# A hybrid decoder step on one core: a third bank for the scores, the sample spread evenly, and TensorE's order fixed to the order of emission

## The chip, the core and the metric

The kernel runs on one core of a Trainium2 chip. A core has five engines with instruction queues of their own: TensorE (PE, matrix products; its weight loads are listed as PEld), VectorE (DVE), ScalarE (ACT), GpSimd (POOL) and SyncE (SP, which here issues nearly all DMAs). PE writes into eight PSUM banks of 128 x 512 float32 values; VectorE and ScalarE read them. The metric is the time of one execution on the device in microseconds (us).

## What is computed

One inference step: a recurrent layer, shared keys and values made from its result, then one layer of forgetting attention. It is done for a prompt of 2048 new positions and for 8 samples of 8 new positions each that look back on 4096 cached positions in pages.

```python
def fox_block(q, k, v, cq, ck, q_pos, k_pos):
    s = jnp.einsum('bqhd,bkhd->bhqk', q, k).astype(jnp.float32) * (HEAD_DIM ** -0.5)
    s = s + jnp.swapaxes(cq, 1, 2)[:, :, :, None] - jnp.swapaxes(ck, 1, 2)[:, :, None, :]
    mask = k_pos[None, :] <= q_pos[:, None]
    s = jnp.where(mask[None, None], s, -jnp.inf)
    p = jax.nn.softmax(s, axis=-1)
    return jnp.einsum('bhqk,bkhd->bqhd', p.astype(v.dtype), v)
...
def run_group(...):
    x = x + rms_norm(recurrent_mixer(rms_norm(x, ...), ...), ...)
    k_new, v_new, logf_new = shared_kv(x, kv_norm, w_kv, b_f)
    ...
    x = x + rms_norm(fox_mixer(rms_norm(x, ...), k_all, v_all, cq, ck, ...), ...)
```

There are 16 heads of 64 values; the model is 1024 wide. The sample reads 8 x 32 pages of 128 rows, keys and values, from a pool through a page table.

## The kernel before

Three stages follow each other: the recurrent layer, the projections to keys, values, queries and gates, and the attention of the prompt with the output projection behind it. The first 1024 positions pass the first two stages, then the rest. Beside the later projections and the attention runs the *sample*, the attention of the eight samples over cached pages. It is cut into 16 turns (a batch entry and half of the heads); the first two are done early, the other 14 by the generator `beside`.

The attention of the prompt (`attention`) goes through 64 units of a head and 512 queries. A unit has one *score* step per 128 keys, 640 in all. A step has two matmuls into a bank named st (L1531, L1532), on the diagonal a third that adds the mask (L1534). ScalarE takes the exponential of the bank (L1540) into a tile p in SBUF. After four steps the *value products* (ops, L1551) add p times the values into a bank of their own; they are emitted two steps late. GpSimd adds the p tiles up for the sums (L104). The exponential needs the maximum of each query beforehand: *maxima* (sx, L1404) are scores computed ahead of time, from which VectorE takes the largest (L1406; L1408 on the diagonal). mrow is the row of maxima of a unit, and mps its transpose (L1421), which ScalarE writes into the unit's queries (qbt).

A sample turn loads eight groups of four key pages and eight of value pages (L1072; tile raw, four buffers, 1 MB each). VectorE transposes the keys (ktr, L1157), PE makes scores from them (dS, L1125; L1140 for the new rows), VectorE subtracts the decay and takes maxima. At the end of a turn's keys the maximum (dm) is transposed on PE (L1177, L1181), ScalarE takes exponentials (L1194), PE sums them (dsum, L1203), VectorE transposes them (sy, L1210), and SP stores them to DRAM (pd, L1215) and loads them in another layout (sx, L1216). Then the value products of the turn (dO, L1235; L1243 for the new rows) follow page by page, and dres (L1263) folds the result. Key pages of the next turn are emitted between the value pages of this one. (The tile sx of the sample and the bank sx of the maxima share a name.)

PSUM in the attention: two banks belong to the sample (d, for its scores and the small products of the softmax, and o, for dO), six to the attention: one for ops, two for st, three for sx, mps and the products of the sums.

What sets the order. The program emits instructions in one stream. `Side.along` interleaves two generators: for each unit of cost that the attention reports, the sample is advanced by `share` units. A scheduler then orders each engine's queue with a timeline of its own and may put a later emitted instruction ahead of an earlier one that it expects to wait. `together` keeps a group of matmuls behind the group's first; there is no order between groups. With these costs the sample's share along the attention is that of the projections, 0.28; what is then left is emitted behind the attention (`side.upto`).

Of the kernel before, what the change touches and what calls it, by code (L numbers as in the profile page):

```python
# [11 lines left out]
F32 = mybir.dt.float32  # L12
# [8 lines left out]
P = 128  # L21
# [6 lines left out]
H = 16  # L28
# [15 lines left out]
B_ORDER += [("g", c) for c in range(4)]  # L44

SHARE = 1.13
LEAD = 18
RAMP = 8
NS = 3
# [2 lines left out]
AHEAD = 8  # L52
FIRST = 2
NACC = 5
NP = 5
ADD = "G"
OG = 1
NQ = 6
# [14 lines left out]


SYNC = mybir.DependencyInfo(mybir.DependencyClass.Sync, mybir.DependencyReason.DATA)


def f(ap):
# [5 lines left out]
def tile_hawk_fox(  # L84
# [8 lines left out]
    V, A, G, T, S = nc.vector, nc.scalar, nc.gpsimd, nc.tensor, nc.sync  # L93
# [9 lines left out]
    def tt(eng, out, a, b, op):  # L103
        eng.tensor_tensor(out, a, b, op=op)  # L104

    def together(mms, after=()):

        first = mms[0]().ins
        for d in after:
            tc.add_manual_dep(first, d.ins.name, SYNC)  # L110
        with tc.high_priority(), tc.issue_after(first):
            for mm in mms[1:]:
                mm()


    xs_flat = x_sample.rearrange("b q d -> (b q) d")
# [94 lines left out]
    psum = {}  # L211
# [810 lines left out]
    def decode(es, turns, nraw, nktr, ahead):  # L1022
# [26 lines left out]
        last, qbs = [], {}  # L1049

        def bank(name, tag="d"):
            return psum["dec"].tile([P, 512], F32, name=name, tag=tag, bufs=1)

        def spare():
# [252 lines left out]
    def attention(es):  # L1307
# [86 lines left out]
        def top(u, j, ck):  # L1394

            h, qc = units[u]
            assert h in loaded and u < done[1]
            kb, qb = kbs[h % 2], qbs[u % NQ]
            if (j, ck) == (0, 0):
                mxs[u] = small.tile([P, 4, 4], F32, name="mxs", tag="mxs")  # L1400
            mx = mxs[u]
            w = 512 if ck < qc else (j + 1) * P
            ps = ps3.tile([P, 512], F32, name="sx", tag="sx", bufs=3)
            T.matmul(ps[:, :w], qb[0:96, j * P:(j + 1) * P], kb[0:96, ck * 512:ck * 512 + w], start=True, stop=True)  # L1404
            if ck < qc:
                V.reduce_max(mx[:, j, ck:ck + 1], ps[:, :w], axis=AX.X)  # L1406
            else:
                V.tensor_tensor_reduce(ps[:, :w], ps[:, :w], maskb[:, 512 - w:], scale=1.0, scalar=NEG,  # L1408
                                       op0=ALU.add, op1=ALU.max, accum_out=mx[:, j, ck:ck + 1])
            if j == 3 and ck == qc:  # L1410
                later.after(1, lambda: tops(u))
# [108 lines left out]
            yield 300  # L1520
        ops = acc = None
        pair = []
        for u, (h, qc) in enumerate(units):
            load_low(u + 2)
            for k in range(nks[u]):
# [1 line left out]
                qa, qb = qas[u], qbs[u % NQ]  # L1527
                lo = max(0, k - qc * 4) * P
                ks = slice(k * P, (k + 1) * P)
                ps = ps3.tile([P, 512], F32, name="st", tag="st", bufs=2)  # L1530
                T.matmul(ps[:, lo:], ka[:, ks], qa[:, lo:], start=True, stop=False)  # L1531
                T.matmul(ps[:, lo:], kb[:, ks], qb[:, lo:], start=False, stop=(k < qc * 4))  # L1532
                if k >= qc * 4:
                    T.matmul(ps[:, lo:lo + P], identB[:, :], causal[:, :], start=False, stop=True)  # L1534
# [38 lines left out]
                    load_head(h + 1)  # L1573
                yield 4.1 * (512 - lo) * 0.42 + (done[0] - before) * 213

    lent = {}

    rows = [(NSAMP, None, x1s_d[:, :], ys_flat)]
    rows += [(P, t, x1_d[t:t + P], yp_flat[t:t + P]) for t in range(SEQ - P, -1, -P)]
# [2 lines left out]
    def project_ready(es):  # L1582

        pool = sbuf(es, "projw", "right")
        proj["g"] = pool.tile([P, D], F32, name="bpostB")
        S.dma_start(proj["g"][:, :], b_post_norm.broadcast_to([P, D]))
        out = proj["out"] = Out(b_w_out[0], 0).place(pool)
        with ExitStack() as st:
            wpool["st"], wpool["ns"] = sbuf(st, "projs", "right"), 2
            out.fetch()  # L1590
            out.fetch()
            for i in range(8):
                yield 2000
                out.split(i + 1)
# [189 lines left out]
    def beside():  # L1784
        yield from decode(dec, turns[FIRST:], 4, 2, True)
        dec.close()
        yield from project_ready(last)

    side = Side(beside())
# [3 lines left out]
    wkeep.close()  # L1793
    lin.close()
    psum["att"] = banks(att, "psa", 6)
    side.along(attention(att), share)
    side.upto(1e12)
    project(last)
    att.close()
# [36 lines left out]
```

## Time and profile before

| | us |
|---|---|
| median of three runs | 3062.46 |
| runs | 3054.63 to 3064.86 |
| the profiled execution | 3055.27 |
| its span | 3053.6 |
| PE busy in the span | 2827.0 |
| VectorE busy | 1810.2 |
| ScalarE busy | 1269.8 |
| GpSimd busy | 1079.6 |
| attention, first score to last value product | 1725.5 to 2881.2 |
| first and last value product of the sample from 1690 us on | 1692.2 to 2559.9 |

The span runs from the first to the last instruction of one profiled execution. A row of a group gives line, engine, operation, output and inputs with shapes, the count, the busy time and the mean of one, and how long the engine was idle just before, with what ended that. PEclk is the granted share of PE's clock. Matmuls are pipelined, so the next one may start before the one ahead has ended; the distance from start to start tells what one costs. Line numbers are those of the kernel before; in the changed kernel those that the text names stand 16 to 31 lines further down: the scores' two matmuls are L1561 and L1563, the maxima L1420, the value products L1582, the sample's value products L1251.

### The profile page before, as it was taken

To read this page: it belongs to the slowest core of one execution; us is meant where nothing else is said; L and a number is where in the kernel's file an instruction comes from. 1 tells how busy PE (TensorE), PEld (TensorE's weight loads), DVE (VectorE), ACT (ScalarE), POOL (GpSimd) and SP (SyncE) were. 2 spreads that over 40 slices of the span, in tenths; PEclk is the share of its full clock that TensorE was granted. 3 is DMA by queue.
4 is the path that set the end of the run, shared out by engine and by line. 5 is a ranking of instruction groups with operands and counts; after the bars stand their busy time and mean duration, and the time that the engine had idled before them with its cause. 6 is when DMAs were issued, how large, how long until landed. Compare 5 with 4: busy or idle time off the path is not lost.

```text
span 3053.6 us, 60463 instructions
## 1 busy us (share of the span) xinstructions
PE 2827.0 (93%) x21614; PEld 2258.5 (74%) x21614; DVE 1810.2 (59%) x4012; ACT 1269.8 (42%) x2874; POOL 1079.6 (35%) x1199
## 2 busy tenths in 40 slices
PE   6998999999999989998999799899899899999898
PEld 5997789988999978896888456565556565565687
DVE  7876465425357766765555566676767675554344
ACT  4665442222346655433333144343444345455311
POOL 1653201000016532000000366556465557587522
PEclk9999999999999999999999799899999999999999
DMA  4224546788622256999999988999999998323243
GB/s 122 81 85 133 175 125 203 240 268 263 216 83 89 83 185 194 316 320 320 330 311 315 294 274 268 299 275 308 306 298 319 322 297 258 92 65 86 84 145 111
DMA packets 492864, 653.41 MB, mean 214 GB/s; under 512 B 91099, under 2 KB 292828, under 8 KB 485285
## 3 DMA queue, kind: packets, MB, share of 16 engines
q1 hardware_dynamic: 488934, 643.87, 67.1%
q10 hardware_dynamic: 3340, 3.56, 0.5%
q8 instruction: 171, 2.80, 0.4%
q0 software_dynamic: 288, 2.10, 0.2%
q14 instruction: 131, 1.07, 0.1%
HBM read 513.82 MB, written 135.16 MB: 213 GB/s over the span
## 4 chain that ended last, share of the span: by engine, by line
PE 59%; DMA 18%; DVE 9%; ACT 5%; SPq 4%; issue 3%; POOL 2%; DVEq 0%; ACTq 0%; POOLq 0%
PE ops L1551 6%; PE y L368 4%; PE y L366 4%; PE y L367 4%; DMA raw<-in_cache_v_dram 4%; PE kv L366 4%; PE kv L367 4%; PE kv L368 4%; DMA raw<-in_cache_k_dram 4%; PE st L1531 3%; PE sx L1404 3%; PE dO L1235 3%; PE dS L1125 2%; PE st L1532 2%; PE qg L366 2%
## 5 line engine op out<-in xcount | busy, mean ns | idle before, releaser
L104 POOL TENSOR_TENSOR acc<-acc,p 128x512 f32<-128x512 f32 (+3 forms) x576 | 638.7, 1109 | 419.2 <-PE ops L1551 271.1
L1540 ACT ACTIVATE p<-st 128x512 f32<-128x512 f32 (+3 forms) x576 | 289.5, 524 | 404.9 <-PE st L1532 198.8
L1157 DVE STREAM_TRANSPOSE ktr<-raw 128x1024 f32<-128x1024 f32 x256 | 305.7, 1225 | 160.2 <-DMA raw<-in_cache_k_dram 157.8
L1406 DVE TENSOR_REDUCE mxs<-sx 128x1 f32<-128x512 f32 x384 | 253.1, 679 | 119.7 <-PE sx L1404 118.3
L367 PE MATMUL kv<-wl,xh 128*128 128x256 f32 (+3 forms) x1088 | 309.3, 287 | 11.2 <-DVE wl L411 11.0
L366 PE MATMUL kv<-wh,xh 128*128 128x256 f32 (+3 forms) x1088 | 310.8, 290 | 5.9 <-ACT wh L410 5.4
L368 PE MATMUL kv<-wh,xl 128*128 128x256 f32 (+3 forms) x1088 | 309.4, 287 | 0.0
L1531 PE MATMUL st<-qa,ka 128*128 128x512 f32 (+3 forms) x640 | 273.9, 428 | 12.2 <-ACT p L1540 11.0
L1551 PE MATMUL ops<-p,vvt 128*64 128x256 f32 (+1 forms) x2176 | 261.0, 366 | 3.4 <-ACT p L1540 2.8
L1404 PE MATMUL sx<-kbt,qbt 96*128 96x512 f32 (+3 forms) x640 | 236.9, 425 | 26.1 <-DMA qbt<-qd 12.0
L1532 PE MATMUL st<-qbt,kbt 128*128 128x512 f32 (+3 forms) x640 | 239.3, 374 | 0.0
L410 ACT ACTIVATE wh<-wst,gv 128x256 fp32r<-128x256 f32 (+1 forms) x384 | 164.5, 499 | 179.9 <-DMA wst<-in_b_w_in_dram 62.1
L411 DVE SCALAR_TENSOR_TENSOR wl<-wst,gv,wh 128x256 fp32r<-128x256 f32 (+1 forms) x384 | 170.5, 493 | 105.5 <-ACT wh L410 104.0
L1551 PEld LDWEIGHTS ops<-p,vvt 128*64 128x64 f32 x2176 | 161.2, 140 | 92.6 <-issue 22.7
L366 PE MATMUL qg<-xh,wh 128*128 128x384 f32 (+2 forms) x640 | 228.9, 359 | 0.0
L368 PE MATMUL qg<-xh,wl 128*128 128x384 f32 (+2 forms) x640 | 227.4, 356 | 0.0
L367 PE MATMUL qg<-xl,wh 128*128 128x512 f32 (+2 forms) x640 | 226.9, 356 | 0.0
L367 PEld LDWEIGHTS kv<-wl,xh 128*128 128x128 f32 (+1 forms) x1088 | 204.3, 189 | 14.9 <-DVE wl L411 12.6
L366 PEld LDWEIGHTS kv<-wh,xh 128*128 128x128 f32 (+1 forms) x1088 | 204.2, 189 | 12.0 <-ACT wh L410 6.4
L1090 POOL TENSOR_TENSOR qw<-qb,amask 128x128 f32<-128x128 f32 x64 | 29.3, 464 | 509.9 <-PE dS L1125 266.4
L368 PEld LDWEIGHTS kv<-wh,xl 128*128 128x128 f32 (+1 forms) x1088 | 205.6, 189 | 4.1 <-issue 4.1
L1531 PEld LDWEIGHTS st<-qa,ka 128*128 128x128 f32 x640 | 124.0, 194 | 109.9 <-issue 53.0
(297 smaller groups left out, 6370.0 us busy)
## 6 DMA issues: line engine op xcount, KB each, us to landing
raw<-in_cache_k_dram SPq DMA_DIRECT2D x512, 256.0 KB
raw<-in_cache_v_dram SPq DMA_DIRECT2D x512, 256.0 KB
wst<-in_w_kv_dram SPq DMA_DIRECT2D x48, 512.0 KB
wst<-in_b_w_in_dram SPq DMA_DIRECT2D x48, 512.0 KB
xt<-in_x_prompt_dram SPq DMA_DIRECT2D x32, 512.0 KB
wst<-in_a_w_in_dram SPq DMA_DIRECT2D x64, 256.0 KB
out_dram<-kf SPq DMA_DIRECT2D x128, 128.0 KB
sc<-cd SPq DMA_DIRECT2D x16, 1024.0 KB
```

The lines of the kernel that those rows point to most:

```text
L104: eng.tensor_tensor(out, a, b, op=op)
L366: T.matmul(ps, lh(k), rh(k), start=(k == 0), stop=False)
L367: T.matmul(ps, lh(k), rl(k), start=False, stop=False)
L368: T.matmul(ps, ll(k), rh(k), start=False, stop=(k == nk - 1))
L411: V.scalar_tensor_tensor(wl[:, k, :], st[:, k, :], gk, f(wh[:, k, :]), op0=ALU.mult, op1=ALU.subtract)
L1157: V.transpose(t.kts[pp][:, n], raw[:, :, pp * 256:(pp + 1) * 256])
L1404: T.matmul(ps[:, :w], qb[0:96, j * P:(j + 1) * P], kb[0:96, ck * 512:ck * 512 + w], start=True, stop=True)
L1406: V.reduce_max(mx[:, j, ck:ck + 1], ps[:, :w], axis=AX.X)
L1531: T.matmul(ps[:, lo:], ka[:, ks], qa[:, lo:], start=True, stop=False)
L1532: T.matmul(ps[:, lo:], kb[:, ks], qb[:, lo:], start=False, stop=(k < qc * 4))
L1540: pair.append((k, lo, p, A.activation(p[:, lo:], ps[:, lo:], AF.Exp)))
L1551: return T.matmul(ops[r * HD:(r + 1) * HD, a0 * P:], vvs[h % 2][:, k, :], p[:, :].rearrange("p (a r c) -> p a r c", a=2, r=2)[:, a0:, r, : ...
```

## The change

Three things change, all in the attention stage.

The scores get a third bank. While the sample runs, every third score takes the sample's bank d; the sample's own small tiles move into the rotation of the three sx banks. Once the sample has ended (`dec_done`), every second score takes one of the banks d and o in turn. A sixth buffer for p is added.

The share of the sample along the attention is computed from what is left of it and from the attention's whole cost, so that it is spread over 0.88 of that cost.

From the start of the attention the scores, the maxima, and the groups of value products and sample products that go through `together` are chained: each one's first matmul gets an edge without a semaphore to the one emitted before it, so the scheduler issues them on PE in exactly the order of emission. Transposes (mps, dm) and the products of the sums, dsum and dres are not in the chain.

```diff
 SHARE = 1.13
+SPAN = 0.88
...
-NP = 5
+NP = 6
...
+ORDER = mybir.DependencyInfo(mybir.DependencyClass.NoSync, mybir.DependencyReason.DATA)
...
+    line = []
+
+    def behind(ins):
+
+        if line:
+            if line[0] is not None:
+                tc.add_manual_dep(ins, line[0].name, ORDER)
+            line[0] = ins
+
     def together(mms, after=()):
 
         first = mms[0]().ins
         for d in after:
             tc.add_manual_dep(first, d.ins.name, SYNC)
+        behind(first)
         with tc.high_priority(), tc.issue_after(first):
             for mm in mms[1:]:
-                mm()
+                last = mm().ins
+        if line:
+            line[0] = last
...
         def bank(name, tag="d"):
+            if tag == "d" and "att" in psum:
+                return psum["att"].tile([P, 512], F32, name=name, tag="sx", bufs=3)
             return psum["dec"].tile([P, 512], F32, name=name, tag=tag, bufs=1)
...
-            T.matmul(ps[:, :w], qb[0:96, j * P:(j + 1) * P], kb[0:96, ck * 512:ck * 512 + w], start=True, stop=True)
+            behind(T.matmul(ps[:, :w], qb[0:96, j * P:(j + 1) * P], kb[0:96, ck * 512:ck * 512 + w], start=True, stop=True).ins)
...
+        wide = [0]
+
+        def scores_bank():
+
+            if dec_done:
+                wide[0] += 1
+                if wide[0] % 2:
+                    return psum["dec"].tile([P, 512], F32, name="st", tag="do"[wide[0] // 2 % 2], bufs=1)
+            else:
+                wide[0] += 1
+                if wide[0] % 3 == 0:
+                    return psum["dec"].tile([P, 512], F32, name="st", tag="d", bufs=1)
+            return ps3.tile([P, 512], F32, name="st", tag="st", bufs=2)
...
-                ps = ps3.tile([P, 512], F32, name="st", tag="st", bufs=2)
-                T.matmul(ps[:, lo:], ka[:, ks], qa[:, lo:], start=True, stop=False)
+                ps = scores_bank()
+                first = T.matmul(ps[:, lo:], ka[:, ks], qa[:, lo:], start=True, stop=False)
+                behind(first.ins)
...
         yield from decode(dec, turns[FIRST:], 4, 2, True)
         dec.close()
+        dec_done.append(True)
         yield from project_ready(last)
...
-    side.along(attention(att), share)
+    line.append(None)
+    cost = sum(4.1 * 0.42 * (512 - max(0, k - qc * 4) * P) + 213 for qc in range(4) for k in range(4 * qc + 4)) * H
+    side.along(attention(att), ((16 - FIRST) * TURN - side.spent) / (cost * SPAN))
```

What this does to the order on PE is shown at two places. In names, the number behind a tile tells which one it is.

The first place is around the 150th score of the attention, where maxima of one unit (with the queries qbt0) stand among scores. PE before:

```order
L1404 MATMUL sx_22674<-kbt0_19537,qbt0_19538 128x256
L1531 MATMUL st_22841<-qa_22300,ka_21365 128x384
L1532 MATMUL st_22841<-qbt3_19541,kbt1_19545 128x384
L1534 LDWEIGHTS identB_19566
L1534 MATMUL st_22841<-causal_19567,identB_19566 128x128
L1404 MATMUL sx_22691<-kbt0_19537,qbt0_19538 128x512
L1531 MATMUL st_22847<-qa_22300,ka_21365 128x256
L1532 MATMUL st_22847<-qbt3_19541,kbt1_19545 128x256
L1534 LDWEIGHTS identB_19566
L1534 MATMUL st_22847<-causal_19567,identB_19566 128x128
L1404 MATMUL sx_22694<-kbt0_19537,qbt0_19538 128x512
L1404 MATMUL sx_22788<-kbt0_19537,qbt0_19538 128x384
```

PE now, maxima of the same unit:

```order
L1561 MATMUL st_23166<-qa_22496,ka_21626 128x512
L1563 MATMUL st_23166<-qbt2_19540,kbt1_19545 128x512
L1420 MATMUL sx_23173<-kbt0_19537,qbt0_19538 128x512
L1420 MATMUL sx_23176<-kbt0_19537,qbt0_19538 128x512
L1561 MATMUL st_23180<-qa_22496,ka_21626 128x512
L1563 MATMUL st_23180<-qbt2_19540,kbt1_19545 128x512
L1420 MATMUL sx_23185<-kbt0_19537,qbt0_19538 128x128
L1420 MATMUL sx_23188<-kbt0_19537,qbt0_19538 128x512
L1561 MATMUL st_23191<-qa_22496,ka_21626 128x512
L1563 MATMUL st_23191<-qbt2_19540,kbt1_19545 128x512
L1420 MATMUL sx_23196<-kbt0_19537,qbt0_19538 128x512
L1420 MATMUL sx_23199<-kbt0_19537,qbt0_19538 128x256
```

Maxima that stood one by one or in uneven runs stand in pairs, one pair behind each score.

The second place is the last turn of the sample, just ahead of its first value product (the dO whose second input is the reloaded tile sx). PE before, where the sum (dsum) stands ten scores ahead of it:

```order
L1404 MATMUL sx_27965<-kbt1_19545,qbt2_19540 128x512
L1478 MATMUL rp_27968<-r16_19574,sel16_19573 128x512
L1404 MATMUL sx_27992<-kbt1_19545,qbt2_19540 128x512
L1531 MATMUL st_28134<-qa_27615,ka_26933 128x128
L1532 MATMUL st_28134<-qbt0_19538,kbt0_19537 128x128
L1534 LDWEIGHTS identB_19566
L1534 MATMUL st_28134<-causal_19567,identB_19566 128x128
L1235 MATMUL dO_33317<-raw_33327,sx_33275 32x256 x8
```

PE now, where dsum stands only two scores ahead (the dO of the last row is the place itself):

```order
L1582 MATMUL ops_19527<-p_31714,vvt0_19534 64x256 x2
L1561 MATMUL st_31780<-qa_31015,ka_30010 128x384
L1563 MATMUL st_31780<-qbt3_19541,kbt0_19537 128x384
L1565 LDWEIGHTS identB_19566
L1565 MATMUL st_31780<-causal_19567,identB_19566 128x128
L1279 MATMUL dres_31758<-sel_13813,ob_31756 128x16 x4
L1420 MATMUL sx_31786<-kbt1_19545,qbt5_19543 128x384
L1420 MATMUL sx_31789<-kbt1_19545,qbt5_19543 128x512
L1251 MATMUL dO_31765<-raw_31775,sx_31688 32x256 x8
```

From the turn's transposed maximum (dm) to this product 18 scores were issued before and 7 are now; in the nine other turns of the attention 16 to 30 before and 21 to 26 now. The sample's last value product stands behind score 435 of 640 before and behind score 538 now. On the other engines the same instructions follow PE's new order.

More of the change, by code (lines that the diff above doesn't have):

```diff
@@ L1574, in attention @@
                 yield 4.1 * (512 - lo) * 0.42 + (done[0] - before) * 213
-    lent = {}
+    lent, dec_done = {}, []
     rows = [(NSAMP, None, x1s_d[:, :], ys_flat)]
```

## The prediction

> **What bounds the kernel now.** I read the page first (span, the slices), then a table by stage around the attention, the waits of TensorE there, and single places in order of time. Up to the attention the two programs hold the same instructions in the same order on every engine, so only the stretch from 1690 us on is argued.
>
> ```profile
> span 3053.6 us, 60463 instructions
> PE 2827.0 (93%) x21614; PEld 2258.5 (74%) x21614; DVE 1810.2 (59%) x4012; ACT 1269.8 (42%) x2874; POOL 1079.6 (35%) x1199
> ...
> DMA  4224546788622256999999988999999998323243
> ```
>
> TensorE (PE) is busy for 93% of the span. The DMA row stands at 8 or 9 from about 1220 to 2590 us, while most cache pages of the sample stream in.
>
> ```profile
> core 0: us, PE busy (x) PEld busy (x) DVE busy (x) ACT busy (x) POOL busy (x), PEclk, DMA share, GB/s
> ...
> 1755.00:1908.00 153.00, 141.55 (x1341) 90.99 (x1337) 100.55 (x213) 72.36 (x184) 94.98 (x90) 0.99 0.88 269
> 1908.00:2500.00 592.00, 541.66 (x5361) 343.43 (x5360) 404.66 (x818) 238.88 (x612) 321.55 (x315) 0.94 0.97 306
> ...
> 2600.00:2881.00 281.00, 266.81 (x1492) 166.31 (x1488) 123.73 (x279) 134.19 (x301) 196.92 (x176) 0.99 0.27 75
> 2881.00:3053.60 172.60, 159.50 (x678) 128.19 (x676) 76.18 (x241) 32.79 (x75) 43.01 (x35) 0.96 0.40 131
> ```
>
> The attention runs from 1725 to 2881 us. PE is busy for 92% of it while the sample runs beside it and for 95% afterwards. In the 592 us from 1908 on the DMA share is 0.97 and the granted clock 0.94; at a share of 0.88, just before, the clock is 0.99. What can be won is PE's waits and the lost clock, not PE's work:
>
> ```profile
> engine line waited for: us in total, times, longest us
> PE dO L1235 <- DMA raw<-in_cache_v_dram: 21.5, 15, 3.3
> PE sx L1404 <- DMA qbt<-qd: 12.0, 2, 11.5
> PE st L1531 <- ACT p L1540: 11.0, 25, 1.2
> PE sx L1404 <- DVE mxs L1406: 8.0, 14, 2.3
> PE mps L1421 <- DVE mrow L1417: 7.5, 6, 3.8
> PE dO L1235 <- issue: 5.1, 3, 3.5
> ...
> PE dO L1235 <- DMA raw<-in_cache_k_dram: 3.3, 2, 1.7
> PE sx L1404 <- ACT qbt L1423: 3.2, 8, 0.8
> PE dO L1235 <- DMA sx<-pd: 3.2, 3, 1.3
> ...
> PE dm L1177 <- DVE dmx L1175: 2.1, 1, 2.1
> ```
>
> All rows of that view (1690 to 2881 us) add up to 98 us. The sample's value products (dO) wait 33.1 of them, scores (st) for the exponentials that empty their two banks 11.0, maxima (sx) for their readers about 12. Waits of more than about 2 us go with halved clock:
>
> ```profile
> 2428.84 1.08 PE L1235 MATMUL dO<-raw,sx 128*32 128x256 f32 x8 [3.29 <-DMA raw<-in_cache_v_dram]
> ...
> 1941.80:1962.30 20.50, 16.06 (x64) 10.04 (x64) 13.67 (x32) 4.80 (x12) 1.65 (x2) 0.50 0.99 296
> 2426.50:2433.30 6.80, 4.46 (x23) 2.70 (x24) 1.39 (x4) 0.60 (x1) 0.03 (x1) 0.50 0.96 313
> ```
>
> [...]
>
> **The change part by part.** The order of both programs gives positions, the trace prices. Work: each engine keeps its set of instructions.
>
> *Kinds on PE.* A score is float32r; value products and sample products are float32.
>
> ```profile
> 2007.99 0.50 PE L1531 MATMUL st<-qa,ka 128*128 128x512 f32 x1
> 2008.32 0.39 PE L1532 MATMUL st<-qbt,kbt 128*128 128x512 f32 x1
> 2008.55 0.39 PE L1531 MATMUL st<-qa,ka 128*128 128x512 f32 x1
> 2008.78 0.40 PE L1532 MATMUL st<-qbt,kbt 128*128 128x512 f32 x1
> 2009.11 0.64 PE L1235 MATMUL dO<-raw,sx 128*32 128x256 f32 x8
> ```
>
> From start to start a score matmul takes 0.23 us, but 0.33 just after a change of kind and just before one. In the order of the attention neighbours of different kind fall from 665 to 615: 50 x 0.10 = -5. Against it maxima stand more often directly behind each other (228 neighbours before, 314 now); bound from 0 to 86 x 0.1 (as a change of kind), I take +4. Sum -1.
>
> *Third bank for scores.* Before, a score reuses the bank of the last but one; now of the last but two, and of the last but three once the sample has ended. The 11.0 us should go nearly whole. Their weight loads wait more often:
>
> ```profile
> L1531 PEld LDWEIGHTS st<-qa,ka x640: 186/187/353, 1725.1 to 2866.2; 128*128 128x128 f32 x160
> ...
>   ACT p L1540: 54.6, 118
> ```
>
> Most of the 54.6 us lies beside a running matmul, so the gain lies between 5 (half of the visible waits) and 55; I take -17, near the visible 11.0 plus a little of what hides. The sixth p buffer adds nothing of its own; ACT, which would wait for it, has 58% of the span free.
>
> *Sample spread.* The last page product stands behind score 435 of 640 before, behind 538 now.
>
> ```profile
> L1531 PE MATMUL st<-qa,ka x640: 221/412/797, 1725.5 to 2866.4; 128*128 128x512 f32 x160
> ...
> L1235 PE MATMUL dO<-raw,sx x1392: 376/379/637, 1692.2 to 2559.9; 128*32 128x256 f32 x199
> ...
> PE dO L1235 <- issue: 3.5, 1, 3.5
> PE dO L1235 <- DMA raw<-in_cache_v_dram: 2.8, 1, 2.8
> ```
>
> The last two rows are of 1690 to 1725 us alone. Before, those 435 scores took 1725 to 2560 us, 1.92 us each; the other 205 took 321 us, 1.57 each. Now the sample ends after about 538 x 1.82 = 980 us (an estimate that keeps the sum of the rest), so its bytes per second fall by 15%, and the 306 GB/s of the table to about 270, which is the row of 1755 to 1908. The buffers set the demand: a page's buffer is loaded again two value pages later, and between these stand 9 scores (median) before and 12 now, 17 and 22 us. SP's queue is passed in the same sequence of pages, with attention loads further apart. Of the 33.1 us, 6.3 (3.5 and 2.8) fall before the first score and stay. Of the 26.8 left I take -15; ends 0 and -27. I stay near the middle because the stretch with DMA share 0.88 still has page waits.
>
> *Clock.* With 0.99 instead of 0.94 over 592 us the gain is 30 us, the far end; the other is 0. Page and score waits are 38 of the 98 us, so 40%: -12.
>
> *Exact order, last turn.* A turn's maximum (dm) leads through exponentials, transposes, a store to DRAM (pd) and a load (sx) to its first value product:
>
> ```profile
> L1177 PE MATMUL dm<-ident,dmx x1: 273/273/273, 2509.0 to 2509.0; 128*128 128x128 f32 x1
> ...
> L1210 DVE STREAM_TRANSPOSE sy<-sc x8: 390/440/445, 2513.9 to 2518.9; 128x256 f32<-128x256 f32 x8
> L1215 SPq DMA_DIRECT2D pd<-sy x4: 356/422/572, 2519.7 to 2523.4; - x4
> L1216 SPq DMA_DIRECT2D sx<-pd x1: 423/423/423, 2530.1 to 2530.1; - x1
> ...
> 2537.00 1.29 PE L1235 MATMUL dO<-raw,sx 128*32 128x256 f32 x20 [1.00 <-DMA sx<-pd]
> ```
>
> That is 28.0 us, with 18 scores issued meanwhile. In the other turns it is 16 to 30 scores before and 21 to 26 now: about even, taken at nothing (end +10: one us more in each). In the last turn no next turn's keys stand between, and the new order leaves 7 scores: 7 x 1.82 = 12.7 us, and everything on PE queues behind the product. 28.0 - 12.7 = +15; ends +5 (a quicker trip with idle queues) and +18 (3 us of halved clock).
>
> *Exact order, maxima.* Runs of maxima in the order: 224 single, 121 double, 42 triple and 6 longer before; 14 single, 293 double, 7 of four now. Sample scores, too, now take one of the maxima's three banks.
>
> ```profile
> L1157 DVE STREAM_TRANSPOSE ktr<-raw 128x1024 f32<-128x1024 f32 x148 | 177.2, 1226 | 78.2 <-DMA raw<-in_cache_k_dram 75.8 <-DMA raw<-in_cache_v_dram 1.9 <-DMA r<-rs 0.2
> L1406 DVE TENSOR_REDUCE mxs<-sx 128x1 f32<-128x512 f32 x239 | 156.7, 674 | 47.1 <-PE sx L1404 46.5
> ```
>
> The 12 us of waits belong to 169 runs of two or more, 0.07 us a run; 131 more make +10. Ends: 0, and +75 (below).
>
> *Maximum of a turn.* dm now follows the sample's last score group directly in three turns; the 2.1 us row times two: +4 (0 to +10).
>
> *Taken at nothing:* 66 projection matmuls pass from the attention to behind it (0.23 us each, 15 us, the same PE time in another place; end +15 if they filled waits). The output weights are loaded and split after the sample: 102 scores, 160 us, cover it; without cover their eight copies would be some 10 us.
>
> Sum: -1 - 17 - 15 - 12 + 15 + 10 + 4 = -16 us. Against the profiled execution (3055.3 us, span and 1.7 around it) that is 3039; it lies 7 us under the median 3062.46, so I forecast 3046.
>
> **The rivals.** *VectorE (DVE) becomes the pace of double maxima (slower).* In a step with two, DVE needs 2 x 0.674 = 1.35 us plus the sample's share, while PE spends 1.57 us without sample. A transpose of 1.226 us, or one that waits for its page (75.8 us in all), ahead of a reduction then stops PE, with every score behind it. At 0.25 us in each of 300 runs it is +75 in place of +10: -16 + 65 = +49, 3111. It cancels the gain from 26 / 300 = 0.09 us a run on. For it: DVE's readers sit behind page waits in one queue. Against: only 8.0 us of waits for L1406 so far.
>
> *Page waits stay.* DMA is still near 0.9 of its time, and the forced products stand where they are emitted. Without -15 and -12: +11, 3073.
>
> *The larger gain.* The clock as at 1755 (-30), all 27 us of page waits, maxima free (0): -1 - 17 - 27 - 30 + 15 + 4 = -56, 3006.
>
> *Order of little effect.* PE is in order either way and its work the same; gains and new waits cancel, 3062. [...] Clock cuts here follow waits for data, while two or three banks are cycled already. [...]
>
> **How the numbers follow.** Forecast 0.45, slower DVE pace 0.27, page waits stay 0.13, larger gain 0.09, little effect 0.06. About 0.3% (9 us) is what a measurement here can tell from no change. Faster: 0.38 of the forecast, 0.09, 0.01: 0.48. Same: 0.06 + 0.01 + 0.03 + 0.05 = 0.15. Slower: 0.01 + 0.26 + 0.10 = 0.37. The forecast's own range is 3022 to 3062; the 8-in-10 range reaches to the rivals, 2998 to 3108.
>
> **What would show it.** Right: no wait of st for ACT above 2 us in all, dO waits under 20 us, pages until about 2700, clock 0.96 or more, and one PE wait of over 10 us for sx<-pd in the last turn. Wrong: maxima that wait over 30 us for DVE, or page waits as before; or dO waits at each turn's first product, which would mean that 21 to 26 scores don't cover the trip to DRAM.

## The result and the profile after

The changed kernel takes 3254.78 us (median of four runs, 3252.54 to 3257.55) where the kernel before took 3062.45: 1.0633 times as long, 95% interval 1.0611 to 1.0655. The forecast was 3046, the range ended at 3108. The change is 192 us slower.

The head of the page of the kernel after:

```profile
span 3250.6 us, 60523 instructions
...
PE 2879.3 (89%) x21614; PEld 2284.3 (70%) x21614; DVE 1802.8 (55%) x4012; ACT 1270.5 (39%) x2874; POOL 1081.7 (33%) x1199
...
DMA  4225458697422559999996866776767778664243
```

The span grew by 197 us: PE is busy for 52 us longer with the same 21614 matmuls, and idle for 145 us longer (371.3 us of its span, 226.6 before). No other engine has more to do. In the DMA row the run of eights and nines that marked the sample's stretch before is gone: sixes to eights, over a longer time.

The same table by stage as in the prediction; the last row is the attention without the sample:

```profile
core 0: us, PE busy (x) PEld busy (x) DVE busy (x) ACT busy (x) POOL busy (x), PEclk, DMA share, GB/s
1728.00:1908.00 180.00, 152.21 (x1289) 93.59 (x1293) 103.79 (x223) 67.87 (x174) 84.08 (x84) 0.90 0.66 203
1908.00:2500.00 592.00, 470.35 (x4121) 295.05 (x4113) 315.64 (x642) 202.40 (x498) 283.49 (x275) 0.89 0.73 224
2500.00:2910.00 410.00, 349.50 (x2941) 215.59 (x2942) 212.57 (x456) 156.07 (x391) 206.27 (x193) 0.90 0.76 228
2910.00:3053.00 143.00, 131.59 (x769) 82.55 (x768) 66.92 (x147) 78.07 (x170) 114.32 (x97) 0.98 0.33 93
```

In the 592 us from 1908 on, PE issued 5361 matmuls before and 4121 now. Its busy share fell from 0.91 to 0.79, the clock from 0.94 to 0.89, the DMA share from 0.97 to 0.73. Once the sample has ended (2908 us), things are nearly as before: clock 0.98, PE at 92%, and 101 scores in 144 us, 1.43 us each (1.57 before). So the loss lies in the stretch in which both stand in one order. PE's waits from 1690 to 3080 us:

```profile
PE sx L1420 <- DVE mxs L1422: 62.0, 30, 6.9
PE rp L1494 <- DMA r<-rs: 33.2, 7, 9.6
PE dm L1193 <- DVE dmx L1191: 27.4, 8, 8.7
PE mps L1437 <- DVE mrow L1433: 20.8, 13, 6.6
PE sx L1420 <- DVE mxs L1424: 19.4, 10, 8.3
PE ops L1582 <- ACT p L1571: 18.9, 34, 3.0
...
PE dO L1251 <- issue: 4.6, 1, 4.6
...
PE st L1561 <- ACT p L1571: 1.8, 2, 1.2
PE dO L1251 <- DMA raw<-in_cache_v_dram: 1.2, 2, 0.9
```

The two kinds of wait that the change was priced by are gone: scores for the exponentials 1.8 us (11.0 before), sample products for value pages 1.2 (21.5). In their place stand maxima that wait for VectorE's readers, 81.4 us in 40 waits, and waits at the gate (rp), at dm, mps and the value products, another 100 us. They are long, nearly 2 us on average and up to 9.6. One of them, in order of time:

```profile
2338.00 0.62 PE L1420 MATMUL sx<-kbt,qbt 96*128 96x512 f32 x2
...
2339.55 0.50 PE L1561 MATMUL st<-qa,ka 128*128 128x512 f32 x1
2339.89 0.40 PE L1563 MATMUL st<-qbt,kbt 128*128 128x512 f32 x1
2340.13 0.23 PE L1420 MATMUL sx<-kbt,qbt 96*128 96x128 f32 x1
...
2342.30 2.37 DVE L1173 STREAM_TRANSPOSE ktr<-raw 128x1024 f32<-128x1024 f32 x2 [4.42 <-DMA raw<-in_cache_k_dram]
2344.59 1.25 DVE L1422 TENSOR_REDUCE mxs<-sx 128x1 f32<-128x512 f32 x2
...
2345.30 0.79 PE L1420 MATMUL sx<-kbt,qbt 96*128 96x512 f32 x1 [4.95 <-DVE mxs L1422]
...
2346.32 0.63 PE L1563 MATMUL st<-qbt,kbt 128*128 128x512 f32 x1
```

By 2340.4 three maxima fill the three banks. Their readers stand in VectorE's queue behind two key transposes, which wait 4.42 us for their page and then take 2.37. The fourth maximum waits 4.95 us, and with it every score in the fixed order. Behind the wait a score's second matmul takes 0.63 us where it took 0.40, at a granted clock of 0.50 (2345.3 to 2347 us). Of all 57 waits of over 0.5 us that VectorE ended in the attention (145.7 us, added up from the trace; before 18 waits, 26.7 us), VectorE spent 58 us in key transposes and stood 38 us for key pages ahead of them.

From this the first theory was: pages come late, VectorE stands, maxima stop. The experiments keep one half of it.

### The profile page after: what moved, and what is told of

The parts are those of the page before. It is cut to its first block, busy times and chain, and to the rows that moved or that the text cites. A ratio compares the mean times of both kernels' runs of the same rounds, so it can differ in the third digit from the quotient of the medians.

```text
span 3250.6 us, 60523 instructions
## 1 busy us (share of the span) xinstructions
PE 2879.3 (89%) x21614; PEld 2284.3 (70%) x21614; DVE 1802.8 (55%) x4012; ACT 1270.5 (39%) x2874; POOL 1081.7 (33%) x1199
## 5 line engine op out<-in xcount | busy, mean ns | idle before, releaser
L1582 PE MATMUL ops<-p,vvt 128*64 128x256 f32 (+1 forms) x2176 | 283.8, 390 | 13.0 <-ACT p L1571 12.5
L1420 PEld LDWEIGHTS sx<-kbt,qbt 96*128 96x128 f32 x640 | 125.2, 209 | 190.9 <-DVE mxs L1422 99.6
L1582 PEld LDWEIGHTS ops<-p,vvt 128*64 128x64 f32 x2176 | 173.2, 150 | 110.9 <-ACT p L1571 30.3
```

The costliest lines, as they stand in the source:

```text
L1420: behind(T.matmul(ps[:, :w], qb[0:96, j * P:(j + 1) * P], kb[0:96, ck * 512:ck * 512 + w], start=True, stop=True).ins)
L1582: return T.matmul(ops[r * HD:(r + 1) * HD, a0 * P:], vvs[h % 2][:, k, :], p[:, :].rearrange("p (a r c) -> p a r c", a=2, r=2)[:, a0:, r, : ...
```

## Experiments

**Which part costs.** Seven kernels take the three parts (exact order, bank, spread) one at a time and in combinations; all keep the sixth buffer for p.

The exact order taken out, bank and spread kept:

```diff
-    line.append(None)
```

> The kernel after without the exact order: third bank for the scores and the even spread stay, TensorE's groups are issued in the scheduler's own order. If the exact order makes the loss (theory): 3020 to 3060 us, TensorE's waits of maxima (sx) for VectorE's reductions fall from the 81 us after to under 25, the key-page waits of VectorE fall from 152 us to under 90. If the maxima's banks being shared with the sample's tiles make it: 3180 to 3260 us, waits of sx for mxs stay above 50 us. If the spread does (pages later beside scores): above 3150 us with the page waits as after.

The bank taken out, order and spread kept:

```diff
-                ps = scores_bank()
+                ps = ps3.tile([P, 512], F32, name="st", tag="st", bufs=2)
...
-            if tag == "d" and "att" in psum:
-                return psum["att"].tile([P, 512], F32, name=name, tag="sx", bufs=3)
```

> The kernel after with the banks of before: the sample's tiles have a bank of their own again and the scores two; exact order and spread stay. If the exact order alone makes the loss: 3230 to 3290 us (the score waits of 11 us come back), waits of sx for mxs stay above 60 us. If sample tiles that stand in the maxima's three banks make it together with the order: 3060 to 3150 us and waits of sx for mxs under 30 us.

The exact order alone: that edit, and the share of before in place of the spread:

```diff
-    side.along(attention(att), ((16 - FIRST) * TURN - side.spent) / (cost * SPAN))
+    side.along(attention(att), share)
```

> Exact order alone: banks and share of before. With the share of before and the work issued as it is emitted, the sample's last products stand behind the last score of the attention. If the exact order makes the loss through pages that come late: 3200 to 3350 us, with VectorE's waits for key pages above 120 us. If it needs the bank or the spread to lose: within 3040 to 3100 us.

The spread alone (neither `line.append(None)` nor the bank):

> Even spread alone: banks and the scheduler's own order as before. After without the exact order (bank and spread) stood at 3148. If the spread makes that remaining loss, because each cache page now stands among more of the attention's own loads and stores in SyncE's one queue: 3120 to 3180 us, DMA share in the sample's stretch below 0.85. If the bank makes it (sample tiles in the maxima's banks): 3040 to 3080.

The bank alone (no exact order, share of before):

> Third bank for the scores alone: share and order of before. If the spread makes the loss that remains without the exact order: 3045 to 3075 us, as before. If the sample's tiles in the maxima's banks make it: 3110 to 3180.

Of the bank only the move of the sample's tiles; the scores keep two banks:

```diff
-                ps = scores_bank()
+                ps = ps3.tile([P, 512], F32, name="st", tag="st", bufs=2)
```

> Of the bank's part only the move of the sample's tiles into the maxima's three banks; scores keep two banks, the freed bank lies idle until the sample has ended; share and scheduler's order as before. The third bank alone took 3230 us. If the move of the sample's tiles makes that loss (the rotation ties the sample to the maxima's emitted places, the scheduler can no longer run it ahead): 3200 to 3270 us, the last page product after the last score. If the scores' use of the freed bank makes it: 3050 to 3100 us.

All three parts, but the sample's groups left out of the order, by a flag that only the attention's value products pass:

```diff
-        behind(first)
+        if chain:
+            behind(first)
...
-        if line:
+        if line and chain:
             line[0] = last
```

> The kernel after, with only the attention's scores, maxima and value products in the exact order; the sample's groups are placed by the scheduler. If the loss comes from the sample's groups being fixed (raw buffers freed late, pages asked for late, VectorE standing at a key page): 3030 to 3090 us, VectorE's waits for key pages under 90 us. If the fixed pairs of maxima alone make VectorE the pace: above 3180 us, and waits of sx for mxs above 60 us although the page waits have gone.

| kernel | median, us | ratio to before, interval |
|---|---|---|
| spread | 3066.09 | 1.0017, 1.0001 to 1.0034 |
| bank | 3229.96 | 1.0551, 1.0511 to 1.0590 |
| of the bank, only the sample's move | 3173.03 | 1.0373, 1.0327 to 1.0419 |
| order | 3301.27 | 1.0778, 1.0731 to 1.0826 |
| spread and bank | 3147.55 | 1.0278, 1.0231 to 1.0325 |
| spread and order | 3233.19 | 1.0556, 1.0512 to 1.0600 |
| spread, bank, order without the sample's groups | 3199.29 | 1.0445, 1.0401 to 1.0489 |
| all three | 3254.78 | 1.0633, 1.0611 to 1.0655 |

Each ratio goes by the kernel before in the same series of runs; its medians there lie between 3059 and 3062 us.

Order and bank each lose, alone and together, and do not add up; that neither expectation for the kernel without the order held (it came between) is the first sign that there are two causes.

The bank alone, too, stood beyond both ranges (3230), and the sample's move between them (3173), since both halves of the bank cost. The move makes 113 us. The scores' use of the freed bank makes another 57, although the scores themselves wait less. The first row is from the kernel with the move alone, the second from that with the whole bank:

```profile
PE st L1561 <- ACT p L1571: 16.3, 38, 1.6
...
PE st L1561 <- ACT p L1571: 3.2, 9, 0.7
```

Against these 13 us, the waits of maxima for the two reductions rise from 10.7 to 31.9 us, those of dO for value pages from 100.0 to 116.9, and the clock over the attention falls from 0.95 to 0.92. Why scores with three banks set this off, no run takes apart.

With the sample's groups out of the order the kernel wins back 55 us (3254.78 to 3199.29), as the second theory for it had it; but the waits of maxima for reductions are 40.3 us there, under the 60 that this theory named, and dO waits 47.6 us for value pages again.

The spread alone changes next to nothing, and one row says why. The sample's value products in the kernel with the spread alone:

```profile
L1249 PE MATMUL dO<-raw,sx x2048: 376/379/636, 646.7 to 2579.6; 128*32 128x256 f32 x187
```

They end at 2580 us (2560 before). In the order on PE the last one stands behind score 439 of 640 (435 before), though by its share it is emitted about a hundred scores later. In the kernel before, with the share that leaves a part of the sample behind the whole attention, it stands at 435 as well: the scheduler had pulled the sample forward to the pace of the DMA engines (share 0.97). With the old share and either the bank, the sample's move or the order, the last product stands behind score 640, with the spread and one of them at 538 to 545. So both parts take the same freedom away: the order by its edges, the bank by the rotation, whose tiles the sample takes in turn with the maxima. Beside either of them the spread is worth something, 82 us with the bank (3230 to 3148) and 68 with the order (3301 to 3233).

What the move alone costs, by stage, the last row behind the last score:

```profile
core 0: us, PE busy (x) PEld busy (x) DVE busy (x) ACT busy (x) POOL busy (x), PEclk, DMA share, GB/s
1725.00:2560.00 835.00, 769.26 (x6343) 483.82 (x6341) 503.03 (x1075) 376.25 (x918) 517.66 (x494) 0.95 0.72 217
2560.00:2793.00 233.00, 210.68 (x1703) 132.42 (x1706) 131.83 (x282) 108.82 (x264) 157.62 (x148) 0.96 0.65 199
2793.00:2946.00 153.00, 74.63 (x1025) 48.23 (x1019) 56.79 (x99) 12.54 (x44) 7.33 (x12) 0.65 0.87 291
```

The DMA engines idle beside the attention (0.72 and 0.65), and for 153 us behind it the sample is alone: PE busy for half of it, at a clock of 0.65. PE's idle time in that tail is 78 us; the kernel's span is 118 us longer than before. With the spread there is no tail, and the bank still costs about 81 us over the spread alone.

**Late pages, or VectorE's place in the order?** Four kernels on the first theory, all made from the kernel after. Its keys without waiting: the transposes of the attention's stretch read a tile that is always there.

```diff
-                    V.transpose(t.kts[pp][:, n], raw[:, :, pp * 256:(pp + 1) * 256])
+                    if "att" in psum:
+                        V.transpose(t.kts[pp][:, n].rearrange("p a (b c) -> p a b c", b=2),
+                                    ident[:, :].unsqueeze(1).unsqueeze(1).to_broadcast([P, 4, 2, P]))
+                    else:
+                        V.transpose(t.kts[pp][:, n], raw[:, :, pp * 256:(pp + 1) * 256])
```

> The kernel after, but during the attention the sample's key transposes read a tile that is always there instead of the page (the pages are still loaded; the sample's scores are then of other keys). VectorE never stands at a page. If the maxima wait because VectorE stands at key pages: 3060 to 3150 us and waits of sx for the reductions under 30 us (81 after). If pairs of maxima alone make VectorE the pace: above 3200 us and these waits above 60 us.

It took 3243.99 us (1.0597, 1.0559 to 1.0634), 11 us less than the kernel after. The expectation of the first theory is off by 94 us and more; the maxima still wait 74.2 us for the reductions. One place in it:

```profile
2073.46 4.62 DVE L1174 STREAM_TRANSPOSE ktr<-ident 128x1024 f32<-128x1024 f32 x4
...
2073.96 0.48 PE L1424 MATMUL sx<-kbt,qbt 96*128 96x512 f32 x1
...
2078.00 0.54 DVE L1428 CUSTOM_DVE_ANT_0 sx<-sx,maskb 128x384 f32<-128x384 f32 x1
...
2078.64 0.80 PE L1424 MATMUL sx<-kbt,qbt 96*128 96x512 f32 x1 [4.20 <-DVE mxs L1428]
```

Transposes that no longer wait come four in a row, 4.62 us, and the reader of the maximum stands behind them as before. In 132 us of waits for VectorE (47 of over 0.5 us), 75 are now spent in transposes. The late page only changes what VectorE does while PE stands; that the readers stand behind the transposes is what counts.

Transposes of a quarter of the length:

```diff
+                    if "att" in psum:
+                        V.transpose(t.kts[pp][:, n, 0:1], raw[:, 0:1, pp * 256:(pp + 1) * 256])
+                    else:
+                        V.transpose(t.kts[pp][:, n], raw[:, :, pp * 256:(pp + 1) * 256])
...
-                                    kt[:, :, a, blk:blk + 32],
+                                    kt[:, :, 0 if "att" in psum else a, blk:blk + 32],
```

> The kernel after, but during the attention each key transpose of the sample is a quarter as long (it does a quarter of a page, and the sample's scores read that quarter four times; the sample's values are then not the reference's). Reading the keys from a resident tile did not help (3244 us), and there TensorE stood 132 us for VectorE, in 75 us of which VectorE was at these transposes. Theory: VectorE's queue has bursts of transposes ahead of the maxima's readers, at places that do not fit TensorE's fixed order. Then 256 x 3/4 x 1.2 us less work for VectorE leaves stalls on VectorE of 60 to 90 us (146 after) and 3140 to 3200 us. Rival: the fixed order itself, with whatever work on VectorE: above 3220 us.

3190.61 us (1.0431, 1.0354 to 1.0507): 64 us back (of the 256 transposes that the expectation counts, 152 lie in the attention), and the waits for VectorE fall from 146 to 75 us, as the theory of the place in the queue had it. But two thirds of the loss stay, and one wait has grown, at a product that is not in the fixed order itself:

```profile
PE rp L1497 <- DMA r<-rs: 63.2, 8, 14.9
```

VectorE in the order of emission, too (an edge from each of its instructions to the next, as for PE):

```diff
+            def issue(*args, **kw):
+                r = op(*args, **kw)
+                if row:
+                    if row[0] is not None:
+                        tc.add_manual_dep(r.ins, row[0].name, ORDER)
+                    row[0] = r.ins
+                return r
```

> The kernel after with VectorE's instructions of the attention, too, issued exactly in the order the program emits. Theory (VectorE's order, set by the scheduler, does not fit TensorE's fixed one): TensorE's waits of maxima for reductions fall from 81 us to under 40 and the time to 3120 to 3220 us. Rival (what is emitted is itself a bad order: every late page and exponential now stops both engines): above 3250 us.

3303.21 us (1.0799, 1.0751 to 1.0846), 48 us more. PE's waits in it (VectorE's instructions all bear the helper's line):

```profile
PE dS L1162 <- DVE ktr L119: 58.4, 13, 14.0
PE sx L1441 <- DVE mxs L119: 40.3, 43, 4.3
PE dO L1272 <- DMA raw<-in_cache_v_dram: 37.3, 10, 11.5
```

The waits of maxima are halved, but others take their place. Two engines in the emitted order are worse than one; the fault is not that VectorE's order differs from PE's alone.

The free bank in the rotation of maxima and sample tiles (four banks), scores with two:

```diff
+    def four(name):
+        turn4[0] += 1
+        if turn4[0] % 4 == 0:
+            return psum["dec"].tile([P, 512], F32, name=name, tag="d", bufs=1)
+        return psum["att"].tile([P, 512], F32, name=name, tag="sx", bufs=3)
...
-            ps = ps3.tile([P, 512], F32, name="sx", tag="sx", bufs=3)
+            ps = four("sx")
```

> The kernel after with the free bank given to the rotation of maxima and sample tiles (four banks) in place of the scores (two banks again). If TensorE stops because all three banks of that rotation wait for VectorE: 3150 to 3220 us, waits of sx for reductions under 55 us (81 after), score waits for the exponentials back at 10 to 25 us. If it waits for VectorE mostly in other ways (maximum of a turn, mrow, gate): above 3225 us.

3236.68 us (1.0581, 1.0527 to 1.0635).

```profile
PE sx L1428 <- DVE mxs L1430: 32.2, 17, 5.1
PE st L1569 <- ACT p L1579: 27.6, 51, 4.3
...
PE dsum L1227 <- DVE mxs L1432: 13.3, 2, 7.3
```

The sx waits for both reductions fall from 81.4 to 34.5 us, more than the theory asked for, yet the time falls by 18 us only. Other waits take their place: those of scores rise from 1.8 to 27.6, dsum now waits 13.3, and all of PE's waits up to the last score fall from 241 to 231 us. A wait that is taken away in a fixed order need not be time won.

The attention's loads on ScalarE's queue, so that SP, which stands 85 us for query buffers while the sample runs, can ask for pages:

```diff
-        queue[0] = S
```

> The kernel after, with one thing else: during the attention the loads of its queries, keys and values are issued from ScalarE's queue and not from SyncE's, which issues the pages. In the kernel after SyncE stands 85 us for query buffers (qa) while the sample runs. If late pages behind those waits are a main cause: 3100 to 3190 us, VectorE's waits for key pages from 152 to under 110 us, DMA share in the sample's stretch up from about 0.74 to above 0.80. If the fixed order of the sample's products or the pairs of maxima are the cause by themselves: 3230 to 3270.

3320.86 us (1.0848, 1.0808 to 1.0887), slower by 66 us. What SP and PE wait for in it:

```profile
SPq L1088 <- PE dO L1251: 163.0, 32, 13.5
...
PE ops L1581 <- ACT p L1570: 41.2, 42, 6.2
...
ACT p L1570 <- issue: 33.0, 7, 8.3
```

SP no longer stands for queries, and so stands for the page buffers, which the fixed products free (81.2 us in the kernel after, 163.0 here). PE loses its time to ScalarE: waits that ScalarE ends add up to 93 us in place of 24. The last row is idle time of ScalarE ahead of exponentials, 33.0 us, that no releaser in the profile ends (no such row in the kernel after); that the loads in ScalarE's queue make it is likely, but the view doesn't name them. The time lies above both ranges that were expected.

**Pace or place.** The sample back to where the kernel before has it:

```diff
-SPAN = 0.88
+SPAN = 0.71
```

With all three parts, without the order, and without the bank:

> The kernel after with the spread set so that the sample's last page product is emitted behind score 434 of 640, about where the kernel before has it (435), and not behind 539. If what loses is the pace that the emitted order gives the sample (thin spread, DMA share 0.74): 3080 to 3150 us, DMA share in the sample's stretch above 0.88. If fixed places on TensorE lose wherever the sample is put, since whatever is late stops all: 3200 to 3270.

> The same spread (last page product behind score 437) with the bank and without the exact order; with 0.88 it stood at 3148. If the sample's pace makes that loss: 3040 to 3090 us, and the sample ends near 2560 us as before. If the shared rotation of banks by itself does: 3120 to 3170.

> The same spread with the exact order and without the bank; with 0.88 it stood at 3233. Pace theory: 3070 to 3140 us. Fixed places theory: 3190 to 3260.

They took 3226.67 us (1.0533, 1.0500 to 1.0566), 3139.25 (1.0246, 1.0218 to 1.0273) and 3220.77 (1.0514, 1.0480 to 1.0547): 28, 8 and 12 us less than with 0.88. The pace is not the main cause. The first of them over its sample's stretch:

```profile
core 0: us, PE busy (x) PEld busy (x) DVE busy (x) ACT busy (x) POOL busy (x), PEclk, DMA share, GB/s
1728.00:2735.00 1007.00, 822.95 (x7513) 513.68 (x7516) 556.36 (x1147) 350.59 (x889) 461.47 (x452) 0.89 0.79 246
```

The last page product stands behind score 434, and yet it comes at 2735 us, not at 2560: the DMA share reaches 0.79, the clock 0.89. So fixed places cost at this pace of the sample as well as at the slower one.

**Which places.** The maxima alone left out of the order, with all else of the change, and also without the bank:

```diff
-            behind(T.matmul(ps[:, :w], qb[0:96, j * P:(j + 1) * P], kb[0:96, ck * 512:ck * 512 + w], start=True, stop=True).ins)
+            T.matmul(ps[:, :w], qb[0:96, j * P:(j + 1) * P], kb[0:96, ck * 512:ck * 512 + w], start=True, stop=True)
```

> The kernel after, with the maxima alone left out of the exact order (scores, value products and the sample's groups stay in it). If the fixed places of the maxima, with VectorE's transposes ahead of their readers, are the largest part of what the exact order costs: 3140 to 3190 us (without any exact order 3148), waits of sx for reductions from 81 to under 40 us. If any fixed group stops TensorE about as often: 3220 to 3260.

> The same without the bank (the sample's tiles have their own bank, scores two); with the maxima in the order it stood at 3233. Fixed maxima as the cause: 3070 to 3130 us. Any fixed group: 3190 to 3240.

Without the bank the time falls from 3233 to 3100.11 us (1.0131, 1.0092 to 1.0169): 133 of the 173 us that spread and order cost there. Head and waits of that kernel:

```profile
PE 2849.0 (92%) x21614; PEld 2265.2 (73%) x21614; DVE 1797.6 (58%) x4012; ACT 1271.4 (41%) x2874; POOL 1079.6 (35%) x1199
...
PE mps L1435 <- DVE mrow L1431: 22.3, 18, 4.5
PE dO L1249 <- DMA sx<-pd: 16.9, 3, 7.9
PE st L1559 <- ACT p L1569: 15.1, 33, 3.1
PE sx L1418 <- DVE mxs L1420: 13.5, 18, 2.6
...
PE sx L1418 <- DVE mxs L1422: 9.0, 10, 2.0
```

Waits of maxima for the two reductions fall from 92.3 to 22.5 us. With the bank, freeing the maxima brings only 50 us (3205.16; 1.0474, 1.0434 to 1.0514), between the two ranges. Their waits for the reductions halve there, too (81.4 to 41.5 us), but the wait at the gate doubles (33.2 to 67.4) and that of mps rises from 20.8 to 36.6:

```profile
PE rp L1494 <- DMA r<-rs: 67.4, 6, 15.3
PE mps L1437 <- DVE mrow L1433: 36.6, 22, 7.2
```

All these tiles, and the sample's, stand in one rotation of three banks; that this rotation is what holds them is likely, but not shown.

**Is anything of it worth keeping?** The spread, and free banks for scores only once the sample has left them (against the kernel with the spread alone):

```diff
-                ps = ps3.tile([P, 512], F32, name="st", tag="st", bufs=2)
+                ps = scores_bank()
...
-            else:
-                wide[0] += 1
-                if wide[0] % 3 == 0:
-                    return psum["dec"].tile([P, 512], F32, name="st", tag="d", bufs=1)
```

> Only what did no harm alone, together: the spread, and more banks for the scores once the sample has ended and its two banks are free; no exact order, and the sample's tiles keep their own banks. The spread alone stood at 3066 (before 3060). Theory: within 3050 to 3070, since scores wait little after the sample. If score waits are worth more than they show: 3030 to 3050.

3053.56 us in ten runs against 3060.41 in thirteen of the kernel before: 0.9979, 0.9963 to 0.9994. That is 7 us less than the kernel before, below the 9 us that the prediction took as measurable; the interval of the ratio lies just under 1.

## Why the prediction was wrong

**The step that failed is "Exact order, maxima".** It put the place of a maximum at 0.07 us a run, 10 us in all, from waits in a kernel in which the scheduler chooses these places. In the kernel after maxima wait 81.4 us for the reductions, and freeing them alone is worth 133 us without the bank, 50 with it. The 12 us of before were not what a maximum costs anywhere, but what is left where a scheduler chooses its place (22.5 in the kernel that frees them without the bank).

**The rival with VectorE** (27%, 3111 us) had place and mechanism, a transpose ahead of a reduction that stops PE with every score behind it, and its price of 0.25 us a run: 81.4 us over 314 runs are 0.26. It was still 144 us short. It counted only the maxima, while dm, mps, rp and the value products wait for another 100 us in the kernel after (27.4, 20.8, 33.2, 18.9). Of these the value products' waits follow the order alone: without the bank they are 18.9 as well, without the order 7.5. Those of dm need both parts (2.7 without the bank, 6.9 without the order), and mps waits even longer without the order (32.4). And the rival left out the lower clock behind long waits: the same matmuls keep PE busy for 52 us longer. Nor is VectorE "the pace": it is busy for 55% of the span. What stops PE is in which order VectorE works. The page waits, which the rival named beside the transposes, could go with a gain of only 11 us (3244).

**"Sample spread"** took the new place of the last page product, score 538, for an effect of the share and counted a gain of 15 us. The spread alone leaves it at 439 and the time at 1.0017. The place came from the order and from the shared rotation, which took the scheduler's freedom away. The page waits of dO did go (21.5 to 1.2 us), but those of VectorE for key pages rose from 75.8 to 152.4. (By its own sum the bytes per second would have been 306 x 835 / 980 = 261 and not 270; 224 to 228 were measured.)

**"Third bank for scores"**, -17, failed too. Score waits fell as priced (11.0 to 1.8; with two banks and the exact order they are 23.3), but no time was won by it while the sample runs: where the third bank is added to the sample's move alone, the kernel takes 57 us more (3173 to 3230). And the other half, the sample's tiles in the maxima's banks, was named without a price. It is 113 us alone, with a tail of 153 us behind the attention; with the spread the whole bank costs about 81.

**"Clock"**: expected to rise from 0.94 towards 0.99, a gain of 12; it fell to 0.89. The small waits went, and long ones took their place. The attention of the kernel after has 39 stretches at 0.50, 257 us together, and in each case PE waited over 1 us within the 7 us ahead of it (before: 14 stretches, 87 us). The third score bank is not needed for the low clock: order and spread with two stay low as well.

```profile
1728.00:3049.00 1321.00, 1125.80 (x9183) 690.42 (x9184) 713.18 (x1486) 511.38 (x1238) 690.86 (x651) 0.91 0.69 210
```

The clock is 0.91 over that attention, and 0.90 with three banks. Where the third bank is added to the sample's move alone, the clock falls from 0.95 to 0.92, but waits grow as well, so what a third bank by itself does to the clock is neither shown nor excluded. Of the two stretches at 0.50 in the prediction, that at 1941.8 us begins 0.5 us into a wait of 3.80 us (1941.3 to 1945.1), not behind it. Six waits of 2.1 to 2.9 us in the attention before stand at such stretches, too; in the kernel after, one of 3.03 us (2116.8 to 2119.9) stands at none.

**"Last turn"**, +15 for the trip to DRAM: one wait of 4.6 us. The place was right, the size was not. That PE, slower by then, gave the trip more time is likely, but no run takes it apart.

```profile
2872.67 1.94 PE L1251 MATMUL dO<-raw,sx 128*32 128x256 f32 x16 [4.57 <-issue]
```

**"Maximum of a turn"**, +4, ends 0 and 10: dm waits 27.4 us in eight waits, beyond the far end. dm is in no chain, but the groups around it are, and its tile stands in the shared rotation.

What stays open: why the gate's product (rp) waits so long (33 us in the kernel after, 63 with short transposes, 67 with free maxima, 17 without the bank, 7 with the spread alone, 0.6 before); why a third bank for the scores costs 57 us; and how the loss with the shared rotation, 79 to 81 us with a spread sample and without the exact order, divides between VectorE's waits and value pages (75.5 and 32.9 us of PE waits over 0.5 us in the kernel with 0.71, 26.7 and 18.0 before).

## What to carry to other kernels

A small wait in the profile of a scheduled kernel is no price for its instruction at a fixed place (for maxima here 0.07 us a run before, 0.26 after): price a fixed order by what else stands ahead of the readers in the other engine's queue, instruction by instruction, and count that everything behind the first late one stops with it (4.95 us at the maximum shown above). Tiles of two streams in one rotation of buffers are an order as well (113 us for that alone here); before putting them together, ask which stream the scheduler had let run ahead (here the one that fills the DMA engines, to a share of 0.97). Take the parts of a change one by one: here the spread did nothing alone but 68 and 82 us beside the others, and only the spread with free banks after the sample's end gained anything (7 us).

## What was unexpected of the hardware

When VectorE's transposes no longer waited for pages, next to nothing was won (11 us of 192): they came four in a row, and PE waited 4.20 us behind 4.62 us of work, much as it had behind a wait of 4.42 us. And moving loads to a queue with idle time (ScalarE, 39% busy) made the kernel 66 us slower: SP's wait went over to buffers that PE frees (81 to 163 us), and PE waited 93 us for ScalarE in place of 24.
